# A mixture-of-experts layer on one core: one gather in the single-pass format from a split x1, and the third expert at 64 rows

## The chip, the cores and the metric

The kernel runs on one core of one Trainium2 chip. The metric is the device time of one execution in microseconds (us). A profiled execution gives a trace, in which times count from the span's start.

## What is computed

The reference is one layer of a streaming encoder: 256 tokens of width 2048, in float32. A token mixer (input projection, gating, pooling, attention, output projection) gives x1. The second half is a mixture of 16 experts, and the change lies at its entrance:

```python
mod = silu(c) @ w_ada + b_ada          # shift, scale, gate, twice
x = x + g1 * token_mixer(rms_norm(x, g_mix) * (1 + sc1) + sh1)        # x1
h = rms_norm(x, g_ffn) * (1 + sc2) + sh2
eidx, gw = route(h, w_router, b_router)      # 1 group of 4, top 2 of its experts
hid = silu(h[rows] @ w_gate[e]) * (h[rows] @ w_up[e])
x = x + g2 * sum over the token's two experts of gw * (hid @ w_down[e])
```

With 256 tokens and two experts each there are 512 assignments. The routing of these inputs by the reference gives the experts, in falling order, 77, 70, 62, 59, 56, 33, 30, 27, 26, 16, 15, 14, 12, 11, 4 and 0 of them.

## The kernel before, in words

TensorE multiplies, ScalarE and VectorE empty its banks and make the small things, GpSimd helps with splits, and SyncE issues the loads of all weights in program order. Each engine, and SyncE's queue, works its own instructions in order.

**Weights.** They stream through a ring of tiles. Up to the routing a ring tile half is 1 MB. For the experts, `wide()` hands out six whole tiles of 2 MB in turn: four old ones (`ring`, three; `ringm`, one) and two new ones (`ringl`), which lie where constants and work tiles of the earlier stages were. An expert is 12 loads of 2 MB: eight for gate and up (`up_stage`), four for down (`down_stage`). A load waits until TensorE, or whoever split the tile, is done with what the tile held.

**Matmul formats.** A plain float32 matmul shows as two records in the trace. In the other way each operand is written as a high part, rounded to a format that TensorE multiplies in a single pass (`F32R`), and a low part, the difference: `split` (line 173) makes the high part by a ScalarE copy and the low part by a subtraction on VectorE or GpSimd, and `mm3` multiplies three of the four pairs.

**Routing** (lines 946 to 1036). When x1 is there, lines 949 to 982 find each token's two experts by some thirty short VectorE instructions on 128 partitions, with one exponential on ScalarE (line 950). Then TensorE counts (lines 986 to 993, with the constants `ones` and `stri`), VectorE ranks the experts by their counts, TensorE turns the ranking into an order (line 1018), and VectorE writes that order to `irow` (line 1022). SyncE reads an expert's number from there before each expert's loads. Between these steps TensorE works off the last tiles of the "ada" product of the second gate (`g2_run`, lines 985 and 1019), whose end adds a bias row (`bgt`, line 265) and whose result ScalarE copies out (line 771).

**Ranks and rows.** `CAPS` gives the rows kept for the expert of each rank: three of 128, six of 64, six of 32. `ORDER` gives the order in which the ranks are worked: 9, 0, 3, 10, 1, 4, 11, 2, 5, 12, 6, 7, 13, 8, 14. An expert of 128 rows uses the split format, its weights split on ScalarE and VectorE as they land; one of 64 or 32 rows uses plain matmuls on two or four column groups of TensorE. If an expert has more tokens than its rows, a second loop at the end (line 1342) runs it again with 128 rows, without any load ahead.

**Gather** (lines 1063 to 1086, 1322). All 512 assignments are gathered by a one-hot product: `oneh` is 256 tokens by 512 slots, scaled by the token's norm `rs1`; for each of 16 column blocks of x1 two plain matmuls (one per 128 tokens) give 128 columns by 256 slots, and ScalarE or VectorE writes them with scale and shift to `XT`. It is done in two halves of 256 slots: one at line 1086, one at line 1322, right before the first expert. `oneh` lies in the last tile of the expert ring. After the first half stand four products that spread the second gate (line 1140), and VectorE's tables of rows and weights (lines 1089 to 1135).

Of the kernel before, what the change touches and what calls it, by code (L numbers as in the profile page):

```python
# [11 lines left out]
F32 = mybir.dt.float32  # L12
F32R = mybir.dt.float32r
I32 = mybir.dt.int32
PSUM = bass.MemoryType.PSUM
AF = mybir.ActivationFunctionType
OP = mybir.AluOpType
# [4 lines left out]
T, D, FE, NE = 256, 2048, 1024, 16  # L22
KD = D // 128
# [17 lines left out]

CAPS = [128] * 3 + [64] * 6 + [32] * 6 + [0]
ORDER = [9, 0, 3, 10, 1, 4, 11, 2, 5, 12, 6, 7, 13, 8, 14]


RING, RING_MORE, RING_LAST = 3, 1, 2
RINGW = 2048
# [66 lines left out]
def body(tc, x_d, prm_d, bg_d, wada_d, win_d, wout_d, egu_d, ed_d, out_d):  # L116
    nc = tc.nc
    root = ExitStack()
    root.enter_context(tc.manual_schedule())

    def pool(name, bufs=1, side=None, space=None):
        s = ExitStack()
        kw = {} if space is None else {"space": space}
        p = s.enter_context(tc.tile_pool(name=name, bufs=bufs, side=side, **kw))
        return p, s

    cst, s_cst = pool("cst")
    ringp, s_ring = pool("ring")

    wides = [ringp.tile([128, 2 * RINGW], F32, name=f"ring{i}") for i in range(RING)]  # L130

    halves_of = []
# [5 lines left out]
    ring_tiles = deque(x for t in wides for x in parts_of(t))  # L138
# [28 lines left out]
    V, S, G, E = nc.vector, nc.scalar, nc.gpsimd, nc.tensor  # L167

    def mm(out, lhsT, rhs, start=True, stop=True):
        E.matmul(out, lhsT=lhsT, rhs=rhs, start=start, stop=stop, skip_group_check=True)  # L170


    def split(hi, lo, src, eng=None):
        S.copy(hi, src)  # L174
        (eng or V).tensor_tensor(lo, src, hi.bitcast(F32), op=OP.subtract)  # L175
# [7 lines left out]
    c1, s_c1 = pool("c1", 1, side="right")  # L183
# [8 lines left out]
    xa = cst.tile([128, 2, D], F32, name="xa")  # L192
# [36 lines left out]
    def pm():  # L229
        return psM.tile([128, 512], F32, name="pm")  # L230
# [7 lines left out]
    bgt = c1.tile([8, 512], F32, name="bgt")  # L238
# [76 lines left out]
    mod = cst.tile([128, 4, KD], F32, name="mod")  # L315
# [25 lines left out]
    pb, s_pb = pool("pb", 1, side="right")  # L341
# [6 lines left out]
    hp, s_hp = pool("hp", LOOK + 1, side="right")  # L348
# [414 lines left out]
    ring2, s_ring2 = pool("ring2")  # L763
# [48 lines left out]
    o = 0  # L812
    for w in (128, 64, 32, 0):
        n = CAPS.count(w)
        V.memset(capR[:, o:o + n], float(w))
# [123 lines left out]
    rs1 = cst.tile([128, 2], F32, name="rs1")  # L939
# [3 lines left out]
    logit_b(3)  # L943


    B3 = [128, 2, 16]
    sc = rtile(B3, "sc")
    for h in range(2):
        V.scalar_tensor_tensor(sc[:, h, :], lgp[:, h, :], rs1[:, h:h + 1], lconst, op0=OP.mult, op1=OP.add)
    S.activation(sc, sc, AF.Exp, scale=-1.0)  # L950
    V.tensor_scalar(sc, sc, 1.0, None, op0=OP.add)
    V.reciprocal(sc, sc)
    sl = rtile(B3, "sl")
    V.tensor_tensor(sl, sc, par("br")[:, None, :].to_broadcast(B3), op=OP.add)
    s4 = sl.rearrange("p h (g e) -> p (h g) e", g=4)
# [24 lines left out]
    oh2 = first_max(sl, 16, "oh2")  # L980
    M = rtile(B3, "M")
    V.tensor_tensor(M, oh1, oh2, op=OP.add)
# [2 lines left out]
    g2_run(len(g2p) - NG2)  # L985
    pp = pt()
    for h in range(2):
        mm(pp[:, 32:48], ones, M[:, h, :], h == 0, h == 1)
    for h in range(2):
        mm(pp[0:16, 48:49], M[:, h, :], ones[:, 0:1], h == 0, h == 1)  # L990
    mm(pp[:, 0:16], stri, M[:, 0, :])
    mm(pp[:, 16:32], stri, M[:, 1, :], stop=False)
    mm(pp[:, 16:32], ones, M[:, 0, :], start=False)
    SQ = [128, 16, 16]
    tmp = rtile(SQ, "tmp")

# [11 lines left out]
    key = rtile([128, 16], "key")  # L1008
# [25 lines left out]
    start = rtile([128, 16], "start")  # L1034
# [1 line left out]
    pick(start, tmp, cnt)  # L1036


    s_hp.close()
    s_pb.close()  # L1040
    s_c1.close()
    pg2, s_pg2 = pool("pg2", 1, side="right")
    g2w = pg2.tile([128, D], F32, name="g2w")
    wides += [pg2.tile([128, 2 * RINGW], F32, name=f"ringl{i}") for i in range(RING_LAST)]
    old = wides[:RING + RING_MORE]
    used = [max(i for i, x in enumerate(ring_tiles) if x is a or x is b) for a, b in halves_of]
    wide_ring = deque(wides[RING + RING_MORE:] + [t for _, t in sorted(zip(used, old), key=lambda x: x[0])])

    def wide():
        wide_ring.rotate(-1)  # L1050
        return wide_ring[-1]

    XT = pg2.tile([128, KD, 512], F32, name="XT")

    oneh = wide_ring[-1][:, :1024].rearrange("p (h s) -> p h s", h=2)
    sl1 = rtile(B3, "sl1")
    sl2 = rtile([128, 2, 2], "sl2")
    V.tensor_tensor(sl1, pos[:, 0:2, :], start[:, None, :].to_broadcast(B3), op=OP.add)
    t3 = rtile(B3, "t3")
    for i, oh in enumerate((oh1, oh2)):  # L1060
        V.tensor_tensor(t3, sl1, oh, op=OP.mult)
        V.tensor_reduce(sl2[:, i, :], t3, AX.X, OP.add)
    oht = rtile([128, 512], "oht")
    for h in range(2):
        V.tensor_scalar(oneh[:, h, :], io512, sl2[:, 0, h:h + 1], rs1[:, h:h + 1], op0=OP.is_equal, op1=OP.mult)
        V.tensor_scalar(oht, io512, sl2[:, 1, h:h + 1], rs1[:, h:h + 1], op0=OP.is_equal, op1=OP.mult)
        V.tensor_tensor(oneh[:, h, :], oneh[:, h, :], oht, op=OP.add)

    def gather(half, k, bank):

        o = slice(256 * half, 256 * half + 256)
        p = bank()
        for h in range(2):
            mm(p[:, :256], xa[:, h, 128 * k:128 * k + 128], oneh[:, h, o], start=h == 0, stop=h == 1)
        if k % 2 or half == 0:
            S.activation(XT[:, k, o], p[:, :256], AF.Identity, scale=mod[:, 3, k:k + 1], bias=mod[:, 2, k:k + 1])
        else:
            V.tensor_scalar(XT[:, k, o], p[:, :256], mod[:, 3, k:k + 1], mod[:, 2, k:k + 1], op0=OP.mult, op1=OP.add)

    staR = rtile([128, 16], "staR")  # L1080
    stc = rtile([128, 16], "stc")
# [1 line left out]
    V.tensor_tensor(stc, staR, limR, op=OP.min)  # L1083
    V.tensor_copy(irow[:, 32:48], stc[0:1, :])
    for k in range(KD):
        gather(0, k, pm)


    cntR = rtile([128, 16], "cntR")
# [48 lines left out]
    for b in range(4):  # L1138
        p = pm()
        mm(p, sel, r2[b])  # L1140
        S.copy(g2w[:, 512 * b:512 * b + 512], p)
    s_rt.close()
    s_wk2.close()
    s_psT.close()
# [5 lines left out]
    def bank():  # L1150
        return psB.tile([128, 512], F32, name="bank")
# [150 lines left out]
    def tokens(r):  # L1302
        w = CAPS[r]
        s0 = reg(32 + r, [DVE], 512 - w, why)
        return tokens_of(w, s0)

    def tokens_of(w, s0):
# [4 lines left out]
        for a in range(4):  # L1312
            k = slice(4 * a, 4 * a + 4)
            src = XT[:, k, ds(s0, w)]
            if w == 128:
# [3 lines left out]
                V.tensor_copy(xr[:, k, :], src)  # L1319
        return xr  # L1320

    for k in range(KD):
        gather(1, k, bank)
    xr = tokens(ORDER[0])
    for i, r in enumerate(ORDER):
        w = CAPS[r]
        load = make_load(reg(r, [SP], NE - 1, why))
# [29 lines left out]
        hid = up_stage(128, xr, load)  # L1357
        down_stage(128, hid, gt, load, store)()

    for s in (s_pg2, s_ring2, s_ring, s_cst, root):  # L1360
        s.close()


# [41 lines left out]
```

## Time and profile before

| | |
|---|---|
| three runs, us | 1456.87, 1457.91, 1460.44 (median 1457.91) |
| the profiled execution, its own time | 1460.89 us |
| its span, first to last instruction | 1459.1 us |
| TensorE matmuls busy | 1264.6 us, 87% of the span |
| VectorE, ScalarE, GpSimd busy | 693.5, 412.8, 146.0 us |
| moved from and to memory | 539.14 MB, 369 GB/s over the span |
| mean granted TensorE clock | 0.958 |

The page gives busy times, the rate of DMA and the chain of work that ended last, followed back from the last instruction. Windows give the same for a stretch; the timeline gives instructions one by one, with the time that the engine had waited and for whom. PE is TensorE's matmuls, DVE VectorE, ACT ScalarE, POOL GpSimd, SPq the queue in which SyncE issues loads. A busy TensorE is not TensorE at its peak, since matmuls overlap.

### The profile page before, as it was taken

How to read it: one execution, taken by the hardware profiler on the slowest of the kernel's cores; microseconds unless marked ns; L12 is line 12 of the kernel's file. 1: busy time of each engine (PE TensorE's matmuls, PEld its weight loads, DVE VectorE, ACT ScalarE, POOL GpSimd, SP SyncE). 2: the span in 40 equal slices, each digit the busy share in tenths (PEclk: the TensorE clock that was granted, in tenths of full speed). 3: DMA queues.
4: the chain of work that ended last, by engine and by line, in shares of the span. 5: the costliest groups of instructions: out<-in, count | busy, mean ns of one | idle time of the engine just before them, and what ended most of it. 6: DMA issues, size and time to landing. Idle time of an engine off the chain costs nothing.

```text
span 1459.1 us, 17581 instructions
## 1 busy us (share of the span) xinstructions
PE 1264.6 (87%) x6930; PEld 703.1 (48%) x6930; DVE 693.5 (48%) x1184; ACT 412.8 (28%) x720; POOL 146.0 (10%) x89
## 2 busy tenths in 40 slices
PE   5999999999989997999968999789997879858865
PEld 3666666666667563575324753337633222222221
DVE  3757483555798372795125961169711202202112
ACT  4433333646333240583003840028400000000000
POOL 0423332311333100000000000000000000000000
PEclk8999999999999998999999999999999999979988
DMA  9787787888877868998999989999899999999997
GB/s 378 270 348 281 281 340 265 303 351 328 349 278 270 310 288 367 427 428 317 421 426 427 426 318 419 424 428 426 333 408 428 427 426 427 428 426 428 426 426 303
DMA packets 49207, 539.14 MB, mean 369 GB/s; under 512 B 5464, under 2 KB 5592, under 8 KB 7008
## 3 DMA queue, kind: packets, MB, share of 16 engines
q1 hardware_dynamic: 47664, 534.79, 89.7%
q10 hardware_dynamic: 1456, 3.17, 0.6%
q8 instruction: 56, 0.92, 0.2%
q14 instruction: 31, 0.25, 0.0%
HBM read 535.85 MB, written 2.10 MB: 369 GB/s over the span
## 4 chain that ended last, share of the span: by engine, by line
PE 38%; DMA 27%; DVE 5%; issue 1%; ACT 1%; DVEq 0%; ACTq 0%
PE lbank L170 28%; DMA ring<-in_e_down_dram 11%; DMA ringl<-in_e_gu_dram 9%; DMA ring<-in_e_gu_dram 7%; PE bank L170 5%; PE pm L170 3%; DVE grow L292 2%; PE ada L170 1%; DVE whl L175 1%; DVE el L175 1%; ACT el L174 0%; DVE grow L290 0%; PE lgp L170 0%; DVE hid L1225 0%; PE pt L170 0%
## 5 line engine op out<-in xcount | busy, mean ns | idle before, releaser
L170 PE MATMUL pm<-whl,hT 128*128 128x512 f32 x1120 | 300.9, 405 | 19.9 <-DVE whl L175 10.8
L170 PEld LDWEIGHTS pm<-whl,hT 128*128 128x128 f32 x1120 | 212.3, 193 | 93.6 <-issue 15.3
L170 PE MATMUL lbank<-ringl,xr 128*32 128x256 f32 (+1 forms) x1152 | 143.7, 496 | 38.0 <-DMA ringl<-in_e_gu_dram 37.8
L170 PE MATMUL lbank<-el,xs 128*128 128x512 f32 x576 | 139.9, 401 | 10.2 <-ACT el L174 7.4
L170 PE MATMUL lbank<-ring,xr 128*32 128x256 f32 (+1 forms) x864 | 105.6, 491 | 34.1 <-DMA ring<-in_e_gu_dram 34.0
L174 ACT CAST whl<-ring 128x1024 fp32r<-128x1024 f32 x96 | 99.0, 1048 | 125.7 <-PE pm L170 70.7
L175 POOL TENSOR_TENSOR whl<-ring,whl 128x1024 fp32r<-128x1024 f32 x43 | 108.3, 2518 | 231.7 <-ACT whl L174 211.0
L170 PEld LDWEIGHTS lbank<-el,xs 128*128 128x128 f32 x576 | 109.3, 192 | 41.0 <-ACT el L174 10.6
L170 PE MATMUL bank<-y,gt 128*128 128x512 f32 x240 | 119.1, 619 | 0.0
L1284 DVE TENSOR_TENSOR xa<-xa,bank 128x512 f32<-128x512 f32 x120 | 82.5, 687 | 69.9 <-PE bank L170 69.9
L170 PEld LDWEIGHTS lbank<-ringl,xr 128*32 128x32 f32 (+1 forms) x1152 | 51.9, 128 | 129.8 <-issue 68.5
L170 PE MATMUL lbank<-ring,hidT 128*64 128x512 f32 (+1 forms) x576 | 103.8, 624 | 11.5 <-DMA ring<-in_e_down_dram 11.5
L1275 DVE TENSOR_TENSOR y<-lbank,g2w 128x512 f32<-128x512 f32 x60 | 41.5, 691 | 145.7 <-PE lbank L170 145.7
L174 ACT CAST el<-ring 128x512 fp32r<-128x512 f32 x144 | 89.7, 623 | 29.6 <-PE lbank L170 21.7
L175 DVE TENSOR_TENSOR el<-ring,el 128x512 fp32r<-128x512 f32 x144 | 92.7, 688 | 0.0
L175 DVE TENSOR_TENSOR whl<-ring,whl 128x1024 fp32r<-128x1024 f32 x53 | 72.2, 1368 | 35.9 <-ACT whl L174 33.6
L170 PE MATMUL ada<-ring,cact 128*1 128x512 f32 (+1 forms) x648 | 75.1, 566 | 15.6 <-DMA ring<-in_w_ada_dram 14.4
L1171 ACT COPY gt<-bank 128x256 f32<-128x256 f32 x15 | 5.6, 372 | 287.9 <-PE bank L1169 287.9
L170 PEld LDWEIGHTS lbank<-ring,xr 128*32 128x32 f32 (+1 forms) x864 | 39.5, 128 | 98.4 <-DMA ring<-in_e_gu_dram 48.4
L1225 DVE TENSOR_TENSOR hid<-hid,lbank 128x512 f32<-128x512 f32 x12 | 8.2, 687 | 165.0 <-PE lbank L170 164.7
L170 PE MATMUL lbank<-el,hidT 128*128 128x512 f32 x288 | 74.8, 411 | 12.2 <-DVE el L175 8.3
L438 DVE TENSOR_TENSOR z<-z,pm 128x512 f32<-128x512 f32 x72 | 49.0, 685 | 71.8 <-PE pm L170 71.8
(363 smaller groups left out, 1219.3 us busy)
## 6 DMA issues: line engine op xcount, KB each, us to landing
ringl<-in_e_gu_dram SPq DMA_DIRECT2D x60, 2048.0 KB, 20.1
ring<-in_w_ada_dram SPq DMA_DIRECT2D x90, 1024.0 KB, 7.0
ring<-in_e_gu_dram SPq DMA_DIRECT2D x45, 2048.0 KB, 24.4
ring<-in_e_down_dram SPq DMA_DIRECT2D x45, 2048.0 KB, 25.6
ring<-in_w_in_dram SPq DMA_DIRECT2D x35, 1024.0 KB, 7.0
ringm<-in_e_gu_dram SPq DMA_DIRECT2D x15, 2048.0 KB, 21.7
ringm<-in_e_down_dram SPq DMA_DIRECT2D x15, 2048.0 KB, 21.5
ring<-in_w_out_dram SPq DMA_DIRECT2D x12, 1024.0 KB, 8.3
```

The lines of the kernel that those rows point to most:

```text
L170: E.matmul(out, lhsT=lhsT, rhs=rhs, start=start, stop=stop, skip_group_check=True)
L174: S.copy(hi, src)
L175: (eng or V).tensor_tensor(lo, src, hi.bitcast(F32), op=OP.subtract)
L292: eng.scalar_tensor_tensor(a, w[:, j, :], ck, a, op0=OP.mult, op1=OP.add)
L438: V.tensor_tensor(dst, dst, P[h], op=OP.add)
L1171: S.copy(gt, p[:, :256])
L1225: V.tensor_tensor(hid[:, o], hid[:, o], P[2 * b + 1], op=OP.mult)
L1275: V.tensor_tensor(y, P, g2w[:, c0:c0 + 512], op=OP.mult)
L1284: V.tensor_tensor(a, a, p, op=OP.add)
```

## The change

The gather becomes one set of products over all 512 slots in the single-pass format. `split_x` scales x1 by the token norm and splits it in two parts, during the routing: for each of four pieces of 1024 columns ScalarE scales and then copies to the high part, and GpSimd subtracts. The one-hot is then a plain 0 and 1 and needs no split, so a block takes four single-pass matmuls (two parts, two token halves) of 512 columns. ScalarE alone empties them.

For that the closing of the earlier stages' tiles moves ahead of the routing: `XT` and the split x1 (`xhl`) and `oneh` lie where constants and work tiles were. The constants that the routing still needs are copied first (`one2`, `stri2`), and the bias rows are loaded a second time (`bgt2`, on ScalarE's queue). The two new ring tiles `ringl` come only after the gather, where `xhl` was, and the expert loads begin with the four old tiles, the one unused longest first.

The expert of rank 2 has 64 rows, not 128. `ORDER` stays.

```diff
-CAPS = [128] * 3 + [64] * 6 + [32] * 6 + [0]
+CAPS = [128] * 2 + [64] * 7 + [32] * 6 + [0]
...
     rt, s_rt = pool("rt")
+    bgt = rt.tile([8, 512], F32, name="bgt2")
+    nc.scalar.dma_start(bgt, bg_d.rearrange("a (q n) -> (a q) n", n=512))
...
+    one2 = rtile([128, 128], "one2")
+    V.tensor_copy(one2, ones)
+    stri2 = rtile([128, 128], "stri2")
+    V.tensor_copy(stri2, stri)
...
     logit_b(3)
 
+    s_hp.close()
+    s_pb.close()
+    s_c1.close()
+    pg2, s_pg2 = pool("pg2", 1, side="right")
+    g2w = pg2.tile([128, D], F32, name="g2w")
+    XT = pg2.tile([128, KD, 512], F32, name="XT")
+    phl, s_phl = pool("phl", 1, side="right")
+    xhl = phl.tile([128, 2, 2, D], F32R, name="xhl")
+    oneh = phl.tile([128, 2, 512], F32R, name="oneh")
+
+    def split_x():
+        xn = XT[:, 0:8, :].rearrange("p (h a) n -> p h (a n)", h=2)
+        for c in range(2):
+            o = slice(1024 * c, 1024 * c + 1024)
+            for h in range(2):
+                S.activation(xn[:, h, o], xa[:, h, o], AF.Identity, scale=rs1[:, h:h + 1])
+                split(xhl[:, 0, h, o], xhl[:, 1, h, o], xn[:, h, o], G)
...
     V.reciprocal(sc, sc)
+    split_x()
...
-        mm(pp[:, 32:48], ones, M[:, h, :], h == 0, h == 1)
+        mm(pp[:, 32:48], one2, M[:, h, :], h == 0, h == 1)
...
-    mm(pp[:, 0:16], stri, M[:, 0, :])
+    mm(pp[:, 0:16], stri2, M[:, 0, :])
...
-    s_hp.close()
-    s_pb.close()
-    s_c1.close()
-    pg2, s_pg2 = pool("pg2", 1, side="right")
-    g2w = pg2.tile([128, D], F32, name="g2w")
-    wides += [pg2.tile([128, 2 * RINGW], F32, name=f"ringl{i}") for i in range(RING_LAST)]
-    old = wides[:RING + RING_MORE]
-    used = [max(i for i, x in enumerate(ring_tiles) if x is a or x is b) for a, b in halves_of]
-    wide_ring = deque(wides[RING + RING_MORE:] + [t for _, t in sorted(zip(used, old), key=lambda x: x[0])])
...
-    XT = pg2.tile([128, KD, 512], F32, name="XT")
-
-    oneh = wide_ring[-1][:, :1024].rearrange("p (h s) -> p h s", h=2)
...
-    oht = rtile([128, 512], "oht")
     for h in range(2):
-        V.tensor_scalar(oneh[:, h, :], io512, sl2[:, 0, h:h + 1], rs1[:, h:h + 1], op0=OP.is_equal, op1=OP.mult)
-        V.tensor_scalar(oht, io512, sl2[:, 1, h:h + 1], rs1[:, h:h + 1], op0=OP.is_equal, op1=OP.mult)
-        V.tensor_tensor(oneh[:, h, :], oneh[:, h, :], oht, op=OP.add)
-
-    def gather(half, k, bank):
-
-        o = slice(256 * half, 256 * half + 256)
-        p = bank()
+        V.tensor_scalar(oneh[:, h, :], io512, sl2[:, 0, h:h + 1], None, op0=OP.is_equal)
+        V.scalar_tensor_tensor(oneh[:, h, :], io512, sl2[:, 1, h:h + 1], oneh[:, h, :].bitcast(F32),
+                               op0=OP.is_equal, op1=OP.add)
+
+    def gather(k):
+
+        p = pm()
         for h in range(2):
-            mm(p[:, :256], xa[:, h, 128 * k:128 * k + 128], oneh[:, h, o], start=h == 0, stop=h == 1)
-        if k % 2 or half == 0:
-            S.activation(XT[:, k, o], p[:, :256], AF.Identity, scale=mod[:, 3, k:k + 1], bias=mod[:, 2, k:k + 1])
-        else:
-            V.tensor_scalar(XT[:, k, o], p[:, :256], mod[:, 3, k:k + 1], mod[:, 2, k:k + 1], op0=OP.mult, op1=OP.add)
+            for i in range(2):
+                mm(p, xhl[:, i, h, 128 * k:128 * k + 128], oneh[:, h, :], h + i == 0, h + i == 2)
+        S.activation(XT[:, k, :], p, AF.Identity, scale=mod[:, 3, k:k + 1], bias=mod[:, 2, k:k + 1])
...
     for k in range(KD):
-        gather(0, k, pm)
+        gather(k)
...
         S.copy(g2w[:, 512 * b:512 * b + 512], p)
+    s_phl.close()
+    pl, s_pl = pool("pl", 1, side="right")
+    wides += [pl.tile([128, 2 * RINGW], F32, name=f"ringl{i}") for i in range(RING_LAST)]
+    old = wides[:RING + RING_MORE]
+    used = [max(i for i, x in enumerate(ring_tiles) if x is a or x is b) for a, b in halves_of]
+    wide_ring = deque([t for _, t in sorted(zip(used, old), key=lambda x: x[0])] + wides[RING + RING_MORE:])
...
-    for k in range(KD):
-        gather(1, k, bank)
     xr = tokens(ORDER[0])
```

## Rows read from the trace of the kernel before

**Rows 1.** DMA issues of the page: tile, count, KB each, us to landing

```profile
ringl<-in_e_gu_dram SPq DMA_DIRECT2D x60, 2048.0 KB, 20.1
...
ringm<-in_e_down_dram SPq DMA_DIRECT2D x15, 2048.0 KB, 21.5
```

**Rows 2.** Timeline of VectorE in the routing: start, duration, instruction, wait

```profile
502.69 0.18 DVE L951 TENSOR_SCALAR sc<-sc 128x32 f32<-128x32 f32 x1 [0.30 <-ACT sc L950]
...
504.93 0.17 DVE L970 TENSOR_TENSOR gm<-gm,m 128x8 f32<-128x8 f32 x1
...
505.57 0.19 DVE L977 TENSOR_TENSOR sl<-sl,gm 128x32 f32<-128x32 f32 x1
...
512.06 0.19 DVE L1026 COPY pos<-pt 128x48 f32<-128x48 f32 x1
```

**Rows 3.** Timeline of SyncE's queue, from its first expert load

```profile
516.46 0.89 SPq L1292 DMA_DIRECT2D ringl<-in_e_gu_dram  x2
...
518.15 32.77 SPq L1292 DMA_DIRECT2D ring<-in_e_gu_dram  x3
```

**Rows 4.** Waits of SyncE's queue, 505 to 552: total us, times, longest

```profile
SPq L1292 <- PE bank L170: 31.2, 1, 31.2
...
SPq L1292 <- PE ada L170: 3.6, 1, 3.6
```

**Rows 5.** Windows of 5 us: busy by engine, TensorE clock, DMA share, GB/s

```profile
515.00:520.00 5.00, 2.85 (x12) 1.12 (x9) 4.76 (x13) 0.67 (x2) 0.00 (x0) 1.00 0.51 161
...
540.00:545.00 5.00, 5.00 (x24) 3.79 (x23) 1.63 (x3) 1.56 (x3) 0.00 (x0) 1.00 0.51 216
...
550.00:555.00 5.00, 4.73 (x73) 2.67 (x75) 1.58 (x7) 0.94 (x2) 0.00 (x0) 1.00 0.68 236
```

**Rows 6.** Chain that ended last, an expert of 128 and one of 64

```profile
1046.52 5.28 PE lbank L170 x22
...
1062.96 20.77 PE lbank L170 x96
```

**Rows 7.** Windows of 10 us around the end of the rank-2 expert

```profile
1030.00:1040.00 10.00, 9.08 (x36) 6.49 (x36) 8.50 (x15) 6.22 (x10) 0.00 (x0) 1.00 0.97 399
1040.00:1050.00 10.00, 9.08 (x37) 6.53 (x36) 8.49 (x15) 6.24 (x10) 0.00 (x0) 1.00 0.64 241
1050.00:1060.00 10.00, 10.00 (x38) 4.11 (x39) 4.38 (x9) 0.00 (x0) 0.00 (x0) 1.00 0.77 261
1060.00:1070.00 10.00, 10.00 (x50) 3.26 (x46) 0.25 (x1) 0.37 (x1) 0.00 (x0) 1.00 1.01 401
1070.00:1080.00 10.00, 10.00 (x48) 3.29 (x46) 0.00 (x0) 0.00 (x0) 0.00 (x0) 1.00 1.00 424
```

**Rows 8.** Timeline of all engines near 340, in the input projection

```profile
339.51 2.50 POOL L175 TENSOR_TENSOR whl<-ring,whl 128x1024 fp32r<-128x1024 f32 x1 [18.89 <-ACT whl L174]
...
339.86 2.18 DVE L325 SCALAR_TENSOR_TENSOR mod<-mod,prm 128x4 f32<-128x4 f32 x1
```

**Rows 9.** Groups by line: busy and mean ns, then idle before

```profile
L174 ACT CAST whl<-ring 128x1024 fp32r<-128x1024 f32 x96 | 99.0, 1048 | 125.7 <-PE pm L170 70.7 <-DMA ring<-in_w_in_dram 49.2 <-issue 3.0
```

**Rows 10.** Line 325: durations in ns, least, median and most

```profile
L325 DVE SCALAR_TENSOR_TENSOR mod<-mod,prm x9: 160/165/2183, 22.9 to 361.3; 128x4 f32<-128x4 f32 x7, 128x2 f32<-128x2 f32 x2
```

**Rows 11.** Timeline of VectorE near 354

```profile
354.56 1.41 DVE L632 TENSOR_TENSOR z<-z,prm 128x512 f32<-128x512 f32 x1
```

**Rows 12.** Timeline of GpSimd near 354

```profile
353.97 1.45 POOL L556 TENSOR_TENSOR z<-z,hrv 128x512 f32<-128x512 f32 x1 [11.59 <-DVE hrv L338]
355.50 1.60 POOL L632 TENSOR_TENSOR z<-z,prm 128x512 f32<-128x512 f32 x1
```

**Rows 13.** Chain that ended last, the two halves of the gather

```profile
519.18 17.08 PE pm L170 x70
536.27 14.30 PE bank L170 x64
```

**Rows 14.** Windows of 2 us in the first expert

```profile
576.00:578.00 2.00, 0.37 (x4) 0.20 (x8) 1.54 (x4) 0.00 (x0) 0.00 (x0) 0.50 1.04 442
```

More of the change, by code (lines that the diff above doesn't have):

```diff
@@ L987, in body @@
     for h in range(2):
-        mm(pp[:, 32:48], ones, M[:, h, :], h == 0, h == 1)
+        mm(pp[:, 32:48], one2, M[:, h, :], h == 0, h == 1)
     for h in range(2):
-        mm(pp[0:16, 48:49], M[:, h, :], ones[:, 0:1], h == 0, h == 1)
-    mm(pp[:, 0:16], stri, M[:, 0, :])
-    mm(pp[:, 16:32], stri, M[:, 1, :], stop=False)
-    mm(pp[:, 16:32], ones, M[:, 0, :], start=False)
+        mm(pp[0:16, 48:49], M[:, h, :], one2[:, 0:1], h == 0, h == 1)
+    mm(pp[:, 0:16], stri2, M[:, 0, :])
+    mm(pp[:, 16:32], stri2, M[:, 1, :], stop=False)
+    mm(pp[:, 16:32], one2, M[:, 0, :], start=False)
     SQ = [128, 16, 16]
@@ L1036, in body @@
     pick(start, tmp, cnt)
-    s_hp.close()
-    s_pb.close()
-    s_c1.close()
-    pg2, s_pg2 = pool("pg2", 1, side="right")
-    g2w = pg2.tile([128, D], F32, name="g2w")
-    wides += [pg2.tile([128, 2 * RINGW], F32, name=f"ringl{i}") for i in range(RING_LAST)]
-    old = wides[:RING + RING_MORE]
-    used = [max(i for i, x in enumerate(ring_tiles) if x is a or x is b) for a, b in halves_of]
-    wide_ring = deque(wides[RING + RING_MORE:] + [t for _, t in sorted(zip(used, old), key=lambda x: x[0])])
-    def wide():
-        wide_ring.rotate(-1)
-        return wide_ring[-1]
-    XT = pg2.tile([128, KD, 512], F32, name="XT")
-    oneh = wide_ring[-1][:, :1024].rearrange("p (h s) -> p h s", h=2)
     sl1 = rtile(B3, "sl1")
@@ L1141, in body, with wide @@
         S.copy(g2w[:, 512 * b:512 * b + 512], p)
+    s_phl.close()
[4 more added lines that the diff above has]
+    wide_ring = deque([t for _, t in sorted(zip(used, old), key=lambda x: x[0])] + wides[RING + RING_MORE:])
+    def wide():
+        wide_ring.rotate(-1)
+        return wide_ring[-1]
     s_rt.close()
@@ L1358, in body @@
         down_stage(128, hid, gt, load, store)()
-    for s in (s_pg2, s_ring2, s_ring, s_cst, root):
+    for s in (s_pl, s_pg2, s_ring2, s_ring, s_cst, root):
         s.close()
```

## The prediction, before the changed kernel was built

> **What bounds the kernel now.** I read the issues first, then the stretches of DMA, then the chain. From the routing on, the kernel is a stream of 180 weight loads of 2048 KB (15 experts of 12; 120 for the up stages, 60 for the down stages) [rows 1]. Where nothing holds the queue it moves some 427 GB/s, so a load takes 2.097 MB / 0.427 = 4.9 us and an expert 58.9 us. Every us in which the queue stands still before the last load is lost at the end. The transfers stop for two reasons.
>
> The first is the routing. The loads need the expert order, which VectorE writes by 512.25 [rows 2]. The first load leaves only at 516.46 [rows 3], because its tile lies over the constants that TensorE still reads: SyncE waits 3.6 us for the last "ada" product [rows 4]. The first bytes move 1.7 us after the issue (161 of 427 GB/s in 515 to 520, so from 518.1) [rows 5]. Five loads go out, and the sixth waits 31.2 us for the second half of the gather [rows 3, 4], since its buffer holds the one-hot matrix. The five are through at 542.5 (0.51 of 540 to 545), bytes move again at 552.2 (236 of 427 GB/s in 550 to 555) [rows 5]: a hole of 9.7 us.
>
> The second is an expert of 128 rows. Its 288 single-pass matmuls take 5.28 / 22 = 0.24 us each [rows 6], 69 us without what lies between them, more than 58.9. The ring fills and the rate drops. For the expert of rank 2 four windows give 399, 241, 261 and 401 GB/s [rows 7]; missing are (28 + 186 + 166 + 26) / 427 x 10 us = 9.5 us. After it the rate is whole again (424). There are two more such stretches, for ranks 0 and 1, and they stay.
>
> **The rank-2 expert at 64 rows.** It then takes plain matmuls in two column halves: 96 records in 20.77 us, 0.216 each [rows 6], of which an expert has 128 in the up stage and 64 in the down stage: 41.5 us. With the products into x that is under 58.9, so the transfers set its pace; the splits on ScalarE and VectorE go too, and both were off that path. Saved: the whole 9.5. Bounds: 8.2 (the two deep windows alone) and 9.5 plus 0.7 for rounding at the edges.
>
> **The split of x1.** It adds 8 ScalarE instructions of 1024 columns and 4 subtractions on GpSimd of a form that takes 2.4 to 2.5 us [rows 8]; ScalarE's nearest row has 1.05 us for a cast [rows 9]. ScalarE is free when the exponential of the scores ends, just ahead of 502.69, where VectorE's wait for it ends [rows 2]. The first pair is ready 2.1 us later, so GpSimd starts at about 504.85 and runs its four nearly end to end (a pair every 2.1 us, a subtraction every 2.4). Behind the 8 on ScalarE stand the copies of the second gate's rows: 7 us later. Only TensorE's last group of "ada" products waits for those, and it stands behind the order's product in its queue anyway. GpSimd has nothing else queued; SyncE gets no new wait from it.
>
> The cost is on VectorE. While GpSimd ran such a subtraction, from 339.51 to 342.01, a VectorE instruction of 4 columns took 2.18 us and ended with it, at 342.04 [rows 8]; the line's median is 0.165 [rows 10], like the short rows of the routing [rows 2]. At the seam between two GpSimd instructions VectorE gets one through: the one begun at 354.56 ended at 355.97 [rows 11], 0.55 us after GpSimd's first (355.42), though GpSimd's second had begun at 355.50 [rows 12]. So each of the four subtractions lets one waiting instruction pass. At 504.93 the chain stands at L970; L970, L975, L976 and L977 pass at the four ends, and L977, which ended at 505.76 [rows 2], ends at 504.85 + 4 x (2.4 + 0.18) = 515.2. **The order comes 9.4 us later.** Lower bound 0 (no row has a string of four against such short instructions), upper 10.5 (2.5 and 0.2 for each, 0.3 before the first); I take 9.4, since [rows 8] have the same GpSimd form against an instruction of the same size.
>
> **The first loads.** They go to the old ring, whose tiles TensorE leaves before the order or one by one right behind it, sooner than the load ahead of them is through; with the constants copied (one2, stri2) and the bias rows loaded anew, the 3.6 us wait is gone. First issue: 516.46 - 3.6 + 9.4 = 522.3, **5.8 us later** than before.
>
> **The gather and the hole.** Two sets of 64 records (in the 70 of one chain piece, and in the 14.30 us of the next [rows 13]) become one set of 64 matmuls at 0.24 = 15.4 us. The one-hot takes four VectorE instructions in place of six, somewhat longer ones: taken as nothing, bounds 0.7 either way. The gather's first two products can run before the second half of the one-hot is there (0.5 us), so it ends at 519.2 + 9.4 + 15.4 - 0.5 = 543.5. Loads 1 to 4 run from 522.3 + 1.7 = 524.0 to 543.6. Loads 5 and 6 now go where the split x1 was and wait for the last gather matmul: bytes at 543.5 + 0.1 + 1.7 = 545.3, a hole of 1.7. TensorE stands idle for some 9 us before the order's product, the delay. After a shorter idle time it ran at the lower of its two levels (0.50 of 2.4 GHz in 576 to 578, busy 0.37 of 2.00) [rows 14]. If 4 us of the gather or the products before it run so, it ends 2.0 later. Bounds 0 and 5; I take 2.0. The hole is then 3.7, **6.0 us less**. The evacuation to XT moves wholly to ScalarE, one of 512 columns per four matmuls (0.96 us), hidden, since 1024 columns take 1.05 [rows 9]. VectorE's later tables move with the order and are ready when the gather and the four gate products after it end, near 547; load 7 needs the first expert's tile by 553, so they cost nothing unless those 6 us go.
>
> The new small instructions at the head of the output projection (two copies, one 16 KB load) stand beside TensorE's work there: 0 to 0.5, taken as 0.
>
> **Sum:** + 5.8 - 6.0 - 9.5 = -9.7. The profiled execution took 1460.9 us (span 1459.1), which is 3.0 over the median of 1457.9. So 1451.2 on its clock, 1448.2 as a median. With the bounds (order 7.5 to 10.5 late, hole 1.7 to 6.7, expert 8.2 to 10.2) this case alone runs from 1443.6 to 1453.6.
>
> One number decides the expert's term, the rate: 427 GB/s by the rows. The Trainium skill, SBUF — State Buffer, section "A bandwidth-pool intuition that's wrong (but worth ruling out)", gives about 358 GB/s between HBM and one core; by it an expert's loads would take 70.3 us, the 128-row expert would lose nothing, and the sum would be -0.2. Here the rows decide against it.
>
> **The rivals.**
> - *Short hold.* VectorE slips several instructions through each seam, so the order is under 4 us late. For it: no row shows four in a string. Against: [rows 8]. With no delay the first issue is 3.6 earlier, the hole 1.7 (8.0 less), the expert 9.5: -21.1, 1436.8; with 4 us, 1440.8. Chance 0.18.
> - *Nothing back from the expert.* The pace there is set elsewhere, so that the queue's lost 9.5 us turn up again at the ends of the 64-row experts around it. Then only -0.2 is left: 1457.7. Against it: the 41.5 us of such an expert, far under 58.9. Chance 0.12, of which 0.03 is for the loads being no faster than the 128-row expert's matmuls. The page on SBUF named above, with its 358 GB/s, would have it so.
> - *Slower: the gather is late.* Loads 5 and 6 hang on it now, on top of the 9.4. The gain is gone when the hole is 13.4, that is, when the gather ends at 555.2. At the lower level throughout it takes 15.4 more: 1461.6. If the single-pass format ran as the plain one (four passes of 0.223 for each of the 64, by the 64 records in 14.30 [rows 13], 57 us), 1488. Against: the 0.24 of [rows 6] is that format with 512 columns. Chance 0.05 of more than 0.3% slower.
> - *The change doesn't fit the data.* The routing of these inputs by the reference gives 77, 70, 62, 59 rows; a third expert over 64 would cost a further pass of 59 us or more, over 1507. Chance 0.01.
>
> **Numbers.** The forecast has 0.64. A measurement of this kernel can tell about 0.3% (4.4 us) from no change: faster by more 0.82 (forecast and short hold), within it 0.12, slower 0.06. The range 1437 to 1454 takes in nearly all of the short hold and the upper bounds; what it leaves out is mainly the second and third rivals.
>
> **What would show it.** VectorE's short routing instructions of about 2.4 us beside GpSimd's four; the order at 521.6; the first load at 522, to the old ring; loads 5 and 6 with the end of the gather, near 545; two slow stretches of DMA, not three. It is wrong if those instructions stay at 0.2 us, if the gather takes over 20 us, or if a third stretch under 400 GB/s stays.

## The result, and the profile after

The changed kernel takes 1443.55 us (median of six runs, 1440.43 to 1448.69); the kernel before took 1457.39 beside it (six runs, 1454.21 to 1460.44). The ratio is 0.9909, with a 95% interval from 0.9884 to 0.9933: 13.3 us faster, where 9.7 were forecast. The time lies inside the range of 1437 to 1454.

The two profiled executions differ by more: 1440.43 us of own time (span 1438.6) against 1460.89. The last addition into x1 on GpSimd starts at 488.57 in the trace after and at 495.83 in the trace before (rows below). So 7.3 us of the difference lie ahead of the routing, in stages whose work is the same in both but for two small copies and one 16 KB load. In the six experiments below the same moment lies anywhere from 491.2 to 496.6 (492.6 and 496.6 with the entrance of before, 491.2 to 493.2 with that of after), so most of it is scatter; whether a small part belongs to the change can't be told from single traces. All times below are therefore counted from that start, called **x1** here. From x1 to the end of the span the kernel before takes 963.27 us and the one after 950.03: 13.24 less, close to the 13.3 of the medians.

The rate in 40 slices of the span (some 36 us each), from the page of before:

```profile
GB/s 378 270 348 281 281 340 265 303 351 328 349 278 270 310 288 367 427 428 317 421 426 427 426 318 419 424 428 426 333 408 428 427 426 427 428 426 428 426 426 303
```

And from the page after:

```profile
GB/s 391 283 350 305 275 338 267 302 348 327 377 286 259 310 255 428 426 426 333 420 425 427 427 319 420 425 427 427 427 427 426 427 426 428 427 425 428 426 426 296
```

After, from the sixteenth slice on, the stream of weights stands at some 427 GB/s with two dips, 333 and 319. Before, there are three dips (317, 318, 333). TensorE has 35 us less to do (1229.2 us busy) and VectorE 60 (633.5), which is far more than was saved: past the routing, the time goes by how long the queue of loads stands still.

**The routing.** The last addition into x1 and the writing of the order before:

```profile
495.83 1.29 POOL L841 TENSOR_TENSOR xa<-xa,xg 128x512 f32<-128x512 f32 x1 [8.92 <-DVE xg L839]
...
511.88 0.16 DVE L1022 CAST irow<-pt 1x16 int32<-1x16 f32 x1 [0.48 <-PE pt L170]
```

And after: GpSimd's timeline, from the last addition into x1 on, and VectorE's in the routing:

```profile
488.57 1.29 POOL L847 TENSOR_TENSOR xa<-xa,xg 128x512 f32<-128x512 f32 x1 [8.92 <-DVE xg L845]
497.65 9.31 POOL L175 TENSOR_TENSOR xhl<-XT,xhl 128x1024 fp32r<-128x1024 f32 x4 [7.79 <-DVE m L995]
```

```profile
497.69 2.37 DVE L996 TENSOR_TENSOR gm<-gm,m 128x8 f32<-128x8 f32 x1
500.09 2.31 DVE L1001 TENSOR_TENSOR sl<-sl,gm 128x32 f32<-128x32 f32 x1
502.44 2.25 DVE L1002 TENSOR_SCALAR gm<-gm 128x8 f32<-128x8 f32 x1
504.72 2.28 DVE L1003 TENSOR_TENSOR sl<-sl,gm 128x32 f32<-128x32 f32 x1
507.04 0.19 DVE L992 TENSOR_REDUCE m<-sl 128x2 f32<-128x32 f32 x1
...
514.04 0.16 DVE L1048 CAST irow<-pt 1x16 int32<-1x16 f32 x1 [0.69 <-PE pt L170]
```

Four instructions that took 0.17 to 0.19 us each before (two of them stand in [rows 2]) now take 2.25 to 2.37. GpSimd's four run from 497.65 to 506.96, and VectorE gets one instruction through at the end of each. They are the same four lines that the prediction named (L970, L975, L976 and L977 of before). At 507.04, with GpSimd done, the chain is back at 0.19. The order is written at x1 + 25.47; before it was x1 + 16.05, so 9.42 us later.

**The loads.** SyncE's queue, and below it the queue's waits from 500 to 552 (total us, times, longest):

```profile
515.03 0.35 SPq L1308 DMA_DIRECT2D ringm<-in_e_gu_dram  x1
515.88 4.59 SPq L1308 DMA_DIRECT2D ring<-in_e_gu_dram  x3
535.88 0.87 SPq L1308 DMA_DIRECT2D ringl<-in_e_gu_dram  x2
```

```profile
SPq L1308 <- PE pm L170: 15.2, 1, 15.2
...
SPq L1308 <- PE ada L170: 3.4, 3, 2.8
```

The first four loads go to the old tiles, the first at x1 + 26.46 (before: x1 + 20.63). The wait for the second half of the gather, 31.2 us in [rows 4], has become one of 15.2 for the single set of products. The 3.4 us for the "ada" products now lie behind the first load, between loads that follow each other, where the one ahead is still running. The windows of 5 us show what is left of the hole of 9.7 us:

```profile
505.00:510.00 5.00, 0.25 (x2) 0.25 (x2) 4.29 (x13) 0.00 (x0) 1.96 (x1) 0.54 0.00 0
510.00:515.00 5.00, 3.97 (x24) 2.96 (x28) 1.75 (x10) 0.00 (x0) 0.00 (x0) 0.50 0.01 3
515.00:520.00 5.00, 5.00 (x28) 0.72 (x20) 4.66 (x14) 0.00 (x0) 0.00 (x0) 0.59 0.81 265
520.00:525.00 5.00, 5.00 (x24) 3.44 (x21) 4.59 (x18) 3.02 (x5) 0.00 (x0) 1.00 1.02 436
...
535.00:540.00 5.00, 4.32 (x16) 1.94 (x18) 2.44 (x10) 3.80 (x6) 0.00 (x0) 1.00 0.87 308
```

Only the stretch from 535 to 540 lacks anything: 427 - 308 = 119 GB/s over 5 us are 1.4 us at the full rate. The clock (the third number from the right, ahead of the DMA share) stands at 0.54, 0.50 and 0.59 from 505 to 520, TensorE having 0.25 us of work in the 5 us from 505, and is whole again for the gather, 1.00 from 520 on. TensorE's timeline:

```profile
513.93 6.14 PE L170 MATMUL ada<-ring,cact 128*1 128x512 f32 x32
520.00 1.01 PE L170 MATMUL ada<-bgt,ident 8*1 8x512 f32 x2
520.95 14.81 PE L170 MATMUL pm<-oneh,xhl 128*128 128x512 f32 x64
```

The gather takes 14.81 / 64 = 0.231 us per product and ends at x1 + 47.2; the second half of the old gather ended at x1 + 54.7.

**The third expert.** Windows of 10 us where [rows 7] had their dip:

```profile
1030.00:1040.00 10.00, 7.82 (x36) 2.17 (x32) 0.00 (x0) 0.00 (x0) 0.00 (x0) 1.00 1.01 428
1040.00:1050.00 10.00, 7.31 (x32) 2.12 (x32) 0.00 (x0) 0.00 (x0) 0.00 (x0) 1.00 1.00 424
```

The dip at the end of the rank-2 expert is gone, 428 and 424 in place of 241 and 261. The two others stay: adding up what is missing to 427 in every window, the expert of rank 0 loses 8.7 us and that of rank 1 9.7 (9.8 and 10.2 in the trace of before).

### The profile page after: what moved, and what is told of

The parts are those of the page before. It is cut to its first block, busy times and chain, and to the rows that moved or that the text cites. A ratio compares the mean times of both kernels' runs of the same rounds, so it can differ in the third digit from the quotient of the medians.

```text
span 1438.6 us, 17034 instructions
## 1 busy us (share of the span) xinstructions
PE 1229.2 (85%) x6766; PEld 647.0 (45%) x6766; DVE 633.5 (44%) x1074; ACT 361.5 (25%) x621; POOL 158.6 (11%) x93
## 4 chain that ended last, share of the span: by engine, by line
PE 34%; DMA 29%; DVE 6%; issue 1%; ACT 1%; DVEq 0%; ACTq 0%
PE lbank L170 25%; DMA ring<-in_e_down_dram 11%; DMA ring<-in_e_gu_dram 8%; DMA ringm<-in_e_gu_dram 7%; PE bank L170 5%; PE pm L170 3%; DVE grow L292 2%; DMA ringl<-in_e_down_dram 2%; DMA ringl<-in_e_gu_dram 2%; DVE whl L175 1%; PE ada L170 1%; DVE el L175 1%; DVE grow L290 0%; PE pt L170 0%; DVE hid L1241 0%
## 5 line engine op out<-in xcount | busy, mean ns | idle before, releaser
L170 PE MATMUL lbank<-ring,xr 128*32 128x256 f32 (+1 forms) x1216 | 161.8, 515 | 41.7 <-DMA ring<-in_e_gu_dram 41.7
L170 PEld LDWEIGHTS lbank<-ring,xr 128*32 128x32 f32 (+1 forms) x1216 | 57.3, 132 | 138.0 <-issue 69.6
L170 PE MATMUL lbank<-ring,hidT 128*64 128x512 f32 (+1 forms) x416 | 84.7, 718 | 25.8 <-DVE hidT L1259 17.4
L170 PE MATMUL lbank<-ringl,xr 128*32 128x256 f32 (+1 forms) x608 | 79.9, 509 | 31.4 <-DMA ringl<-in_e_gu_dram 31.3
L170 PE MATMUL lbank<-el,xs 128*128 128x512 f32 x384 | 92.8, 400 | 6.6 <-ACT el L174 4.5
L170 PE MATMUL lbank<-ringm,xr 128*32 128x256 f32 (+1 forms) x608 | 75.6, 472 | 24.8 <-DMA ringm<-in_e_gu_dram 24.1
L175 DVE TENSOR_TENSOR whl<-ring,whl 128x1024 fp32r<-128x1024 f32 x53 | 78.8, 1488 | 30.3 <-ACT whl L174 30.0
L170 PE MATMUL ada<-ring,cact 128*1 128x512 f32 (+1 forms) x648 | 77.4, 582 | 14.5 <-DMA ring<-in_w_ada_dram 13.3
L170 PEld LDWEIGHTS lbank<-el,xs 128*128 128x128 f32 x384 | 72.5, 191 | 27.0 <-ACT el L174 6.6
L170 PE MATMUL lbank<-ringl,hidT 128*64 128x512 f32 (+1 forms) x416 | 74.2, 598 | 3.9 <-DMA ringl<-in_e_down_dram 3.9
L170 PEld LDWEIGHTS bank<-y,gt 128*128 128x128 f32 x240 | 41.6, 191 | 72.9 <-issue 70.5
```

## The experiments

Six kernels ran. Each expectation below stands as it was written before its run. The table gives, for all eight traces, times in us after x1; "hole's end" is the issue of the first load that waits for the gather (the sixth in before, e1_cap and e4_oldfirst, the fifth in the others); the ratio is to the kernel before, run on the same chip beside it (its median was 1458.26 beside the first four experiments and 1457.14 beside the last two).

| kernel | order written | first load | hole's end | x1 to end | median | ratio and interval |
|---|---|---|---|---|---|---|
| before | 16.05 | 20.63 | 54.75 | 963.27 | 1457.39 | |
| after | 25.47 | 26.46 | 47.31 | 950.03 | 1443.55 | 0.9909 (0.9884 to 0.9933) |
| only the third expert at 64 rows (e1_cap) | 16.31 | 23.37 | 57.2 | 954.76 | 1449.47 | 0.9933 (0.9908 to 0.9959) |
| only the split gather (e2_gather) | 25.46 | 26.45 | 47.40 | 957.89 | 1450.99 | 0.9953 (0.9927 to 0.9978) |
| subtractions on VectorE (e3_vsplit) | 16.28 | 17.27 | 38.18 | 940.30 | 1436.11 | 0.9848 (0.9796 to 0.9900) |
| old tiles first (e4_oldfirst) | 16.05 | 17.04 | 59.48 | 964.34 | 1460.34 | 1.0015 (0.9987 to 1.0042) |
| eight subtractions on GpSimd (e5_double) | 33.36 | 34.35 | 55.29 | 958.06 | 1452.41 | 0.9960 (0.9945 to 0.9974) |
| split behind the order (e6_late) | 16.05 | 17.04 | 45.99 | 949.42 | 1443.10 | 0.9898 (0.9874 to 0.9922) |

### The two parts alone

The first, the kernel before with the new row counts:

```diff
-CAPS = [128] * 3 + [64] * 6 + [32] * 6 + [0]
+CAPS = [128] * 2 + [64] * 7 + [32] * 6 + [0]
```

> Only the rows of the third expert change (64, not 128), gather and routing as before. Theory of the terms: the third slow stretch of DMA goes and nothing else moves, so the kernel is 9.5 us faster than before (ratio 0.9935), with two stretches under 400 GB/s after the routing in place of three. Rival 1, the lost 9.5 us turn up again around the 64-row experts: no change (0 to 3 us). Rival 2, the rows alone make the whole gain of the change: 13 us (ratio 0.991).

The second, the kernel after with the old ones:

```diff
-CAPS = [128] * 2 + [64] * 7 + [32] * 6 + [0]
+CAPS = [128] * 3 + [64] * 6 + [32] * 6 + [0]
```

> The changed kernel with the third expert back at 128 rows: only the gather, the split and the order of the ring are new. Theory of the terms: the first load goes out 5.8 us later, the hole after the first loads shrinks from 9.7 to 1.3 us, sum 2.6 us faster than before (ratio 0.998), with three slow stretches of DMA. Rival, the new gather is worth nothing because the hold of VectorE eats it: 0. Rival, it makes the whole gain: 13 us.

The expert alone gives 8.5 us in the trace from x1 (954.76 against 963.27) and 0.9933 in the medians, 6.0 to 13.4 us faster. The gather alone gives 5.4 in the trace and 0.9953, 3.2 to 10.6 us faster. Together that is 13.9, against 13.24 for both at once. Such a close agreement is partly luck, since each trace has its own clock in the routing and its own dips behind it; so the stages are taken one by one.

Where the expert's share lies is seen in the second kernel's windows of 10 us, where its third expert of 128 rows ends:

```profile
1030.00:1040.00 10.00, 9.08 (x36) 6.51 (x36) 8.44 (x15) 6.03 (x10) 0.00 (x0) 1.00 0.71 277
1040.00:1050.00 10.00, 10.00 (x37) 3.93 (x38) 4.37 (x8) 0.00 (x0) 0.00 (x0) 1.00 0.78 267
```

277 and 267 against the 428 and 424 of after. Now the time from where the sixth load is through to the end of the span. (The sixth load is taken to be through 1.7 us after the hole's end and 4.9 us more for each load issued then: one where it is the sixth that waits, two where it is the fifth.) The three kernels with three experts of 128 rows take 902.0 (before), 899.0 (e2_gather) and 898.3 us (e4_oldfirst); the five with two take 891.2 (after), 891.0 (e1_cap), 890.6 (e3_vsplit), 891.3 (e5_double) and 891.9 (e6_late). The means are 899.8 and 891.2: the step is worth 8.6 us, with a spread of 3.7 and 1.3 within the groups.

The gather's share is more than its own stretch shows. Up to where the sixth load is through, the second kernel is 2.4 us ahead of before; the other 3 lie behind, in dips that it has in common with before: 26.2 us are missing in its three, 29.5 in those of before, 24.9 in those of e4_oldfirst, whose gather is that of before. So the profiled execution of before was one with deep dips, and these 3 us can't be put down to the gather. But 2.4, like the 2.6 expected, lies just below the interval of the medians, 3.2 to 10.6 us faster: this expectation was too small.

One thing that the trace of before hides bears on that. In e1_cap routing and gather are those of before, and yet its first load leaves 2.7 us later after x1 and its hole ends 2.5 us later. The cause is a group of "ada" products on TensorE, for which SyncE's first load (6.1 us) and VectorE's writing of the one-hot (2.0 us) wait in e1_cap. In the trace of before:

```profile
511.78 3.61 PE L170 MATMUL ada<-ring,cact 128*1 128x512 f32 x32
```

In that of e1_cap, with two windows of 5 us:

```profile
508.84 6.10 PE L170 MATMUL ada<-ring,cact 128*1 128x512 f32 x32
```

```profile
505.00:510.00 5.00, 3.97 (x26) 2.20 (x28) 2.08 (x12) 0.59 (x1) 0.00 (x0) 0.71 0.26 107
510.00:515.00 5.00, 5.00 (x29) 0.77 (x22) 2.68 (x11) 0.00 (x0) 0.00 (x0) 0.61 0.00 0
```

And in that of e3_vsplit, the kernel of the next section:

```profile
508.97 6.12 PE L170 MATMUL ada<-ring,cact 128*1 128x512 f32 x32
```

The granted clock was 1.00 there in the trace of before, and 0.71 and 0.61 in that of e1_cap. The same group takes 5.31 to 6.24 us in all seven other traces. SyncE's wait for it, 3.6 us in [rows 4], grows by the difference. So the trace of before, from which the prediction and the comparison start, is the one without that drop. Against e1_cap, the second kernel is 4.9 us ahead where the sixth load is through, and that lies inside its interval. How the clock stood in the executions of before that were not profiled isn't known, so this is a candidate for the missing 2.5 us and not shown; a gain ahead of x1 is another.

### What holds the order, and what the order costs

Theory: GpSimd's four subtractions hold VectorE, the order comes 9.4 us late by it, and all of that is on the path. The rival: the order's delay lies beside other waits and costs little. Two kernels, one with no subtraction on GpSimd and one with twice as many. The first moves them to VectorE, one to where TensorE counts, one behind the order and two behind the one-hot (their input lies in the other half of XT, so that the gather's first results don't touch it):

```diff
-                split(xhl[:, 0, h, o], xhl[:, 1, h, o], xn[:, h, o], G)
+                S.copy(xhl[:, 0, h, o], xn[:, h, o])
...
+    def low(c, h):
+        o = slice(1024 * c, 1024 * c + 1024)
+        V.tensor_tensor(xhl[:, 1, h, o], xn[:, h, o], xhl[:, 0, h, o].bitcast(F32), op=OP.subtract)
...
     V.tensor_tensor(M, oh1, oh2, op=OP.add)
+    low(0, 0)
...
     V.tensor_copy(pos, pp[:, :48].rearrange("p (a e) -> p a e", a=3))
+    low(0, 1)
...
+    for h in range(2):
+        low(1, h)
```

> The changed kernel with the four subtractions of the split on VectorE, not GpSimd: one right behind the token choice, while TensorE counts, one behind the order, two behind the one-hot. Theory that GpSimd's four instructions hold VectorE's routing by 9.4 us: no routing instruction on VectorE takes over 0.5 us, the order comes 9.4 us sooner after x1 (16.4 us after GpSimd's last addition into x1, not 25.8), the first load 9.4 sooner, the hole about 1.8 us; 8.9 us faster than the changed kernel, 22 faster than before (ratio 0.985). Rival, the order is late for another reason (ScalarE's eight instructions, the early closing of tiles): the order still comes 25 us after x1 and the time stays within 3 us of the changed kernel (ratio to before 0.991).

VectorE's timeline and SyncE's queue of this kernel (x1 at 492.80):

```profile
505.33 1.22 DVE L973 TENSOR_TENSOR xhl<-XT,xhl 128x1024 fp32r<-128x1024 f32 x1
...
509.08 0.16 DVE L1054 CAST irow<-pt 1x16 int32<-1x16 f32 x1 [0.70 <-PE pt L170]
...
509.36 1.20 DVE L973 TENSOR_TENSOR xhl<-XT,xhl 128x1024 fp32r<-128x1024 f32 x1
...
516.46 2.35 DVE L973 TENSOR_TENSOR xhl<-XT,xhl 128x1024 fp32r<-128x1024 f32 x2
```

```profile
510.07 0.35 SPq L1317 DMA_DIRECT2D ringm<-in_e_gu_dram  x1
510.92 4.57 SPq L1317 DMA_DIRECT2D ring<-in_e_gu_dram  x3
530.98 0.87 SPq L1317 DMA_DIRECT2D ringl<-in_e_gu_dram  x2
```

On VectorE a subtraction takes 1.2 us, half of GpSimd's 2.3. The first fits into the time in which TensorE counts (VectorE waits 0.90 us behind it, where after it waits 2.71), the second stands behind the order, the last two are done at 518.81 while the gather runs. The order is back at x1 + 16.28, 9.2 sooner than after; first load and hole's end come 9.2 and 9.1 sooner, the end 9.7. Its median (four runs) is 1436.11, 7.4 under that of after. It is faster than before by its interval; against after, the two intervals, 0.9796 to 0.9900 and 0.9884 to 0.9933, still overlap, and it is the traces that tell them apart.

The second kernel keeps GpSimd and does every subtraction twice:

```diff
                 split(xhl[:, 0, h, o], xhl[:, 1, h, o], xn[:, h, o], G)
+                G.tensor_tensor(xhl[:, 1, h, o], xn[:, h, o], xhl[:, 0, h, o].bitcast(F32), op=OP.subtract)
```

> The changed kernel with each of GpSimd's four subtractions issued twice, so eight in a string. Theory that each lets one held VectorE instruction pass: eight routing instructions of some 2.3 us, the order 34.8 us after GpSimd's last addition into x1 (25.5 in the changed kernel, 16.1 before), the first load another 9.3 us later, and all of it on the path: 9.3 us slower than the changed kernel, some 4 faster than before (ratio 0.997). Rival, the hold is a fixed cost of the early splitting or of ScalarE's part: order and time as in the changed kernel (ratio 0.991).

VectorE's timeline of it, and GpSimd's around 509:

```profile
502.35 2.37 DVE L997 TENSOR_TENSOR gm<-gm,m 128x8 f32<-128x8 f32 x1
504.75 0.19 DVE L1002 TENSOR_TENSOR sl<-sl,gm 128x32 f32<-128x32 f32 x1
504.98 2.22 DVE L1003 TENSOR_SCALAR gm<-gm 128x8 f32<-128x8 f32 x1
507.24 2.29 DVE L1004 TENSOR_TENSOR sl<-sl,gm 128x32 f32<-128x32 f32 x1
509.56 0.19 DVE L993 TENSOR_REDUCE m<-sl 128x2 f32<-128x32 f32 x1
509.78 2.15 DVE L994 TENSOR_TENSOR oh<-sl,m 128x32 f32<-128x32 f32 x1
```

```profile
509.55 2.34 POOL L969 TENSOR_TENSOR xhl<-XT,xhl 128x1024 fp32r<-128x1024 f32 x1
```

Eight instructions of VectorE are held, from 2.15 to 2.37 us each, for eight of GpSimd. The order comes 7.9 us later than after, and the end 8.0 later (958.06 against 950.03; medians 1452.41 against 1443.55). Expected were 9.3 for the order, the length of GpSimd's four more. The eight held instructions take 17.88 us together, where the four of after take 9.21, and four short ones of 0.19 fall away for it: 7.9. The rest of the longer string lies beside instructions that were not held. A reduce is not held at all (509.56, 0.19 us, inside GpSimd's 509.55 to 511.89), and at 504.75 one instruction got in ahead of GpSimd's next.

The Trainium skill, SBUF — State Buffer, section "Who interferes with whom", says that a VectorE instruction with two inputs in SBUF shuts out, or is shut out by, a GpSimd instruction that reads SBUF, whole instruction by whole instruction, while a reduce never is. The trace agrees on both: 2.15 to 2.37 us for the TENSOR_TENSOR rows that met GpSimd, 0.19 for the reduce among them. The TENSOR_SCALAR row, which has one tensor input, was held too (2.22), which that sentence doesn't cover.

Over the three kernels the order lies at 16.28, 25.47 and 33.36 and the end at 940.30, 950.03 and 958.06: about every us of the order is a us at the end (9.2 and 9.7, 7.9 and 8.0), with these rings. The rival falls.

### The first load, or the end of the gather?

In the kernel before, SyncE waits 3.6 us ahead of the first load. The kernel before with the old tiles ahead of the new ones takes that wait away. (It does one thing more: the one-hot now lies in the last new tile.)

```diff
-    wide_ring = deque(wides[RING + RING_MORE:] + [t for _, t in sorted(zip(used, old), key=lambda x: x[0])])
+    wide_ring = deque([t for _, t in sorted(zip(used, old), key=lambda x: x[0])] + wides[RING + RING_MORE:])
```

> The kernel before with one line changed: the expert loads begin with the four old ring tiles, and the two new ones come last, so the one-hot matrix lies in the last new tile. Theory that the end of the gather sets when the transfers go on: the first load goes out 3.6 us sooner (its wait for the last ada product is gone), the hole after the first five loads grows by the same 3.6 us, and the time stays (ratio 1.000, within 0.002). Rival, the 3.6 us wait of the first load is on the path: 3.6 us faster (ratio 0.9975).

SyncE's queue of this kernel (x1 at 496.56), and its longest waits from 500 to 570:

```profile
513.60 0.35 SPq L1292 DMA_DIRECT2D ringm<-in_e_gu_dram  x1
...
518.88 37.49 SPq L1292 DMA_DIRECT2D ringl<-in_e_gu_dram  x2
```

```profile
SPq L1292 <- PE bank L170: 33.7, 1, 33.7
```

The first load leaves 3.6 us sooner, at x1 + 17.04, and the time is the same within its interval (1.0015). The sixth load still waits for the gather's second half, now 33.7 us; it leaves at x1 + 59.48, 4.7 later than before. Of that, 2.5 are a later beginning of the gather: VectorE waits 2.28 us for the "ada" products (5.31 us here) before it may write the one-hot in its new place. The other 2.4 are the gather's first half, 16.05 us for 62 records in place of 13.65, at a lower clock (0.66 from 520 to 530). So the run is not a clean test of 3.6 us alone. What it does show is that the sixth load leaves with the end of the gather, however early the first: while the ring's last buffer hangs on the gather, a sooner first load only makes the hole longer.

The other way round, the changed kernel with the split behind the order, so that the order and the first load are as early as they can be:

```diff
     V.reciprocal(sc, sc)
-    split_x()
...
     flush()
+    split_x()
```

(Its scratch is the other half of XT, as in e3_vsplit.)

> The changed kernel with the whole split, GpSimd's four subtractions included, issued behind the order in place of ahead of it, and its scratch in the other half of XT. Theory that what counts is what GpSimd holds: now it holds VectorE's later tables, not the choice of experts; the order comes 16.3 us after x1, the first load 9.2 us sooner than in the changed kernel, but the gather waits for the first two subtractions and ends at 43 us after x1 (47.2 in the changed kernel), so the transfers go on 4.2 us sooner: 4 us faster than the changed kernel, 17 faster than before (ratio 0.988), and slower than with the subtractions on VectorE. Rival, the end of the gather does not matter, the first load does: 9 us faster than the changed kernel (ratio 0.985).

Timeline of TensorE, of ScalarE, and windows of 5 us (x1 at 491.18):

```profile
516.17 0.80 PE L170 MATMUL pm<-oneh,xhl 128*128 128x512 f32 x1 [2.80 <-ACT xhl L174]
518.66 1.22 PE L170 MATMUL pm<-oneh,xhl 128*128 128x512 f32 x2 [1.69 <-DVE t L1108]
520.98 16.07 PE L170 MATMUL pm<-oneh,xhl 128*128 128x512 f32 x61 [1.10 <-POOL xhl L175]
```

```profile
522.41 0.77 ACT L1083 ACTIVATE XT<-pm,mod 128x512 f32<-128x512 f32 x1
```

```profile
515.00:520.00 5.00, 2.01 (x3) 0.79 (x3) 4.83 (x9) 4.91 (x6) 3.75 (x2) 0.50 1.01 433
520.00:525.00 5.00, 4.02 (x10) 3.15 (x11) 4.90 (x4) 3.93 (x5) 5.00 (x3) 0.50 1.02 436
```

This expectation missed. Order and first load are 9.4 us sooner than after, but the gather ends at x1 + 45.9, not at the 43.0 expected, and the end comes only 0.6 us sooner (949.42 against 950.03; the medians are 1443.10 and 1443.55). The one-hot is ready at 513.56, yet the gather starts at 516.17 and stumbles twice more over the pieces of x1 as they come, its first results are fetched only when ScalarE is through with all eight instructions of the split (522.41), and TensorE, whose clock had fallen before (0.81 from 505 to 510), stands at the lower level, 0.50, from 515 to 525. From first to last product the gather takes 20.9 us, not 14.8. The place of the split decides which of two things is late, the one-hot or the split x1; the end follows the later of them.

## Why the prediction was right, and where its size was off

**The order, + 9.4: right.** Measured 9.42, by the four instructions named, at the four ends named. In e5_double eight are held for eight, though there one more got in ahead of GpSimd.

**The first load, + 5.8: right against this trace.** Measured 26.46 - 20.63 = 5.83: the order's 9.4 less the 3.6 of the wait. Against e1_cap, where that wait is 6.1, it is 3.1: the term took one trace's wait for the kernel's. It did no harm in the sum, because the hole was reckoned from the same first load.

**The hole, 6.0 less: too small.** It was forecast at 3.7 us, and it is 1.3 to 1.4, so 8.4 less. The term that was mis-sized is the 2.0 us allowed for the lower level of TensorE's clock. The lower level came (0.50 to 0.59 from 505 to 520), but the gather ran at full clock, at 0.231 us a product, not 0.24, which gave 0.6 back. What ran at the lower level was the last "ada" group, 7.1 us (6.14 and 1.01, overlapping) in place of 4.6 (3.61 and 1.01 in the trace of before), and most of that lies beside VectorE's making of the one-hot. The one-hot was ready at 520.37, x1 + 31.8, 1.0 us sooner than reckoned: its four instructions took 2.44 us against 3.36 for the six before, which had been taken as nothing. The gather began at 520.95, 0.6 us after that; by the prediction's own reckoning, with two products ahead of the second half of the one-hot, it could have begun 0.5 us before. So the lower clock cost about 1 us by this estimate, not 2.0, and the quicker one-hot paid for it. The gather ended at x1 + 47.2, where the prediction without the allowance had 47.7 and with it 49.7.

Nor is that drop shown to be the price of the late order, as the prediction had it. In e1_cap and e3_vsplit the order comes at x1 + 16.3, with no such idle time ahead of it, and the same group takes 6.10 and 6.12 us. What sets the level there was not found.

**The expert, 9.5 less: right, a little large.** 8.6 by the two groups of kernels, inside the bounds of 8.2 and 10.2. The rate that decides it, 427 GB/s, holds in the windows after (428, 424), and e1_cap is faster by 6.0 to 13.4 us with this step alone. The figure of the Trainium skill, SBUF — State Buffer, section "A bandwidth-pool intuition that's wrong (but worth ruling out)", 358 GB/s between HBM and one core, is passed in these windows by a fifth; the measurement decides.

**The sum.** + 5.8 - 8.4 - 8.6 makes -11.2, where 9.7 were forecast: the hole gave 2.4 more and the expert 0.9 less. The two traces are 13.24 apart from x1 on. In the trace of before the third dip was 0.9 deeper than the 8.6, and the dips of the two other large experts were 1.6 deeper than after, which makes 13.7; the last 0.5 is not accounted for. These 2.5 us are not the change's: the dips of ranks 0 and 1 range from 8 to 10 us over these runs, whichever gather they follow. The 13.3 us of the medians are 2.1 more than 11.2, and 11.2 lies inside their interval (9.8 to 16.9 us faster). A routing of before at the lower clock, as in e1_cap, would account for 2.5; that it was so in the other executions of before is not shown. So the mechanisms came as forecast, and by the stages the size was short by 1.5 us (2.4 less 0.9); the rest of the 3.6 us is not shown to be the change's.

**The rivals.** The short hold is out: four of four were held. "Nothing back from the expert" is out by e1_cap. The late gather is out: it ended at x1 + 47.2, where the gain would have been gone at x1 + 59.4 (555.2 in the time of before). No second pass ran. All five signs of "What would show it" are there, each near its place in time after x1.

## What to carry to other kernels

Before work is moved to an idle engine, ask whom it shuts out: four GpSimd subtractions of 2.3 us held up a chain of 0.2 us instructions by 9.4 us, and on VectorE itself the same four took 4.8 (1.22, 1.20 and 2.35 for two). When a stream of loads stands still, find the release that ends the gap, and price every step by whether it moves that release: in e6_late a first load 9.4 us sooner brought 0.6 us at the end. And take more than one trace of the kernel before when a term is the depth of a dip or a wait behind TensorE: here a dip varied by some 2 us, and one wait by 2.5.

## What the runs showed of the hardware that had not been expected

- A string of GpSimd instructions of 128 x 1024 with two inputs, end to end, passes about one short VectorE instruction at each seam: four held for four in the trace after, eight for eight in e5_double. One of each was a TENSOR_SCALAR with a single tensor input (2.25 and 2.22 us), the others have two. Reduces in the same chain took 0.18 to 0.19 us beside the string; now and then a second instruction gets through, as at 504.75 in e5_double.
- The lower clock level of TensorE lasted, in the trace after, from 505 to 520 (0.54, 0.50, 0.59) with the engine busy for 3.97 and 5.00 us of the last two stretches, and was gone at the gather (1.00). It came without a long idle time as well: in e1_cap the clock was 0.71 and 0.61 in two stretches of 5 us with 3.97 and 5.00 us of work, and in the trace of before, with 5.00 and 3.97 us of work there, it stayed at 1.00. In e6_late the gather itself began at 0.50 and stood there until 525, with 2.01 and 4.02 us of work in 5.
- The same subtraction, 1024 columns from SBUF, took 1.20 to 1.22 us on VectorE alone and 2.33 on GpSimd (9.31 / 4).
